# Stick-breaking attention on one core: TensorE's order written by hand, scores on row halves, masks by TensorE, the sample's queries on partitions

## The chip, the cores and the metric

One core of one Trainium2 chip runs the whole kernel in one launch. The metric is the device time of that launch in microseconds, the median of three runs. All inputs and outputs are float32.

## The reference, cut to what matters

One inference step of a two-layer encoder, for 256 prompt tokens and 32 sample tokens that have a cache of 256 past tokens. D is 1024. Layer 0 mixes with attentions A and B, layer 1 with C; behind each mixer come cross-attention into 256 memory tokens and an MLP of 4096. The change is in C, stick-breaking attention with 16 heads of 64:

```python
def stick_breaking_attend(q, k, v, q_pos, k_pos):
    z = jnp.einsum('bqhd,bkhd->bhqk', q, k) * (HEAD_DIM ** -0.5)
    before = k_pos[None, :] < q_pos[:, None]
    log_keep = jnp.where(before, jax.nn.log_sigmoid(-z), 0.0)
    tail = lax.cumsum(log_keep, axis=3, reverse=True) - log_keep
    w = jnp.where(before, jnp.exp(jax.nn.log_sigmoid(z) + tail), 0.0)
    return jnp.einsum('bhqk,bkhd->bqhd', w.astype(v.dtype), v)

# prompt: q, k, v = split(rmsnorm(h) @ sb_w_in, 3); 256 queries over 256 keys
# sample: 32 queries over the 256 cached keys and the 32 new ones
# then both: h = h + o @ sb_w_out
```

With `sp = softplus(z)`, both kernels use `w = exp(z - (sum of sp over this key and all later ones up to the query))`.

## The kernel before, in words

**Layout and products.** Activations lie transposed, features on the 128 partitions and the T = 288 tokens (256 prompt, 32 sample) along the free dimension, as 8 tiles of 128 features. A weight matrix comes in chunks of 256 columns and all 1024 rows, by two 512 KB loads on SP's queue (`load_chunk`). Each weight is split in two float32r parts: `wh`, a copy by ScalarE (L144) or VectorE (L142), and `wl = raw - wh` on VectorE or POOL (L145). One instruction of either does a piece of STEP[0] row tiles of 256 columns; every STEP[1]th piece's `wl` goes to POOL, every STEP[2]th piece's `wh` to VectorE (0: none). The activations are split likewise into `xh` and `xl` (L197 for the second), and each product is three matmuls, `mm3`: xh·wh (L159), xl·wh (L160), xh·wl (L161). A chunk is 48 of these, 24 into each of two PSUM banks `g` (pool `ps_g`, three banks). There are 960 products of 288 or 256 columns between the first product of layer 1's mixer and its output projection's last: 12 chunks of queries, keys and values, 4 of memory keys for the cross-attention, 4 of the output projection. Other PSUM pools in this stage are `ps_t`, one bank, and `R.s`, four banks `za`, `zb`, `zs`.

**The stage.** Heads are taken in 4 groups of 4; a group has two pairs of heads, one pair on the 128 partitions of a feature tile (head 0 on partitions 0 to 63, head 1 on 64 to 127). `project_qk` makes a group's `qz` and `kT`, scaled by the norm's `rs` as they leave PSUM. `qz` holds each pair twice, with the other head's rows at zero (`m8` is 0.125 on one half of the partitions), so that one matmul on all 128 rows gives one head's scores. `project_v` makes `vT` and turns it (L433, three transposes a pair into `ps_vt` in `ps_t`) into `vt`, keys on partitions, by two copies on ScalarE (L435, L436).

**Attention, prompt** (`attend_c`, for each pair). `qz` and `kT` are split into float32r parts, and the scores are three products of the parts: L578 into `za` (key tile 0, both heads, 512 columns), L579 into `zb` (key tile 1, queries 128 to 255 only, 256 columns). Softplus: Abs, Exp, Ln on ScalarE (L546, L548, L549), then max(z, 0) + that on VectorE (L553). POOL puts zeros where the key isn't before the query (L558). The result is split (`sph` L594, `spl` L596), and the sum over later keys is made by matmuls with `mtrir` (-1 at and below the diagonal) and `monesr` (all -1), added onto the scores that still lie in PSUM (L599 to L601). Exp gives `w` (L603), POOL masks it again, and L473 multiplies it with `vt`, each head on one half of the columns. `put_prompt` splits the result into `oh` and `ol` for the output projection.

**Attention, sample** (once a group). The scores have the keys on partitions: L618 for the two tiles of cached keys, L621 for the 32 new ones, into `zs`. The same softplus on 256 and 128 columns, the mask on POOL, the sum by plain float32 matmuls (L628 to L632), Exp to `ws` (L637), and `pv_sample` (L483).

**What sets the order.** The body calls the steps of the table `ORD_C` one after the other: `M` is `mem_split` (the split of the memory's activations for layer 1), `q`, `p`, `a` are `project_qk`, `project_v`, `attend_c` of a group, `K` is `mem_k`, a head's memory keys with their norm. `TileContext` then schedules the instructions of each engine by a timeline of its own, so the order on the engines is not that of the calls: products stand between attention steps where its timeline put them. Each engine runs its own queue in that order.

Of the kernel before, what the change touches and what calls it, by code (L numbers as in the profile page):

```python
# [8 lines left out]
F32 = mybir.dt.float32  # L9
F32R = mybir.dt.float32r  # L10
# [4 lines left out]
P = 128  # L15
NP_ = 256
# [15 lines left out]
SHE = 0  # L32
ORD_AB = 'qA0 pA0 F qA1 pA1 aA0 qB0 aA1 qB1 M pB0 pB1 aB0 K2 aB1 K0 K3 K1'.split()
ORD_C = 'M q0 q1 p0 a0 q2 p1 a1 q3 p2 a2 p3 a3 K0 K1 K2 K3'.split()
# [4 lines left out]
ZR = 1  # L39
QZB = (3, 3)  # L40
# [5 lines left out]
STEP = {'ab': (2, 4, 0), 'x0': (4, 5, 7), 'm0': (1, 5, 6), 'c': (2, 5, 0), 'x1': (2, 2, 3), 'm1': (2, 5, 0)}  # L46
# [6 lines left out]
def body(ctx: ExitStack, tc: tile.TileContext, i: dict, o: dict):  # L53
# [27 lines left out]
    def phase(kind):  # L81
        if R.stack is not None:
            R.stack.close()
        R.stack = ExitStack()
        R.step, R.pool_every, R.dve_every = STEP[kind]
        R.c = int(kind == "c")
        R.ph = R.stack.enter_context(tc.tile_pool(name="ph_" + kind, bufs=1))
        R.s = R.stack.enter_context(tc.tile_pool(name="s_" + kind, bufs=4 if kind[0] == "c" else 2, space=PS))
        R.m, R.o = ps_t, R.s
# [177 lines left out]
    eye32 = const.tile([P, NS], F32, name="eye32")  # L267
    for a in range(4):
        r = slice(32 * a, 32 * a + 32)
        dve.tensor_copy(eye32[r, :], ident[r, r])  # L270
        dve.tensor_copy(smask[r, NP_:T], bmask[r, P + 32 * a:P + 32 * a + 32])
# [10 lines left out]
    dve.tensor_copy(bdr, bd)  # L282

# [62 lines left out]
    def mem_k(layer, hd, mh, ml):  # L346
# [41 lines left out]
    def project_qk(wname, cq, ck, xh, xl, rs, norm, ko, oidx, ws0=None):  # L388
        qz = R.ph.tile([P, 2, 2, T], F32, tag="qz", name="qz", bufs=QZB[R.c])
        kT = R.ph.tile([P, 2, T], F32, tag="kT", name="kT", bufs=KTB[R.c])  # L390
        for which, chunk in ((0, cq), (1, ck)):
            ws = load_chunk(i[wname][chunk]) if ws0 is None or which else ws0
            pss = gemm2(ws, xh, xl, pool=R.s if FIRST_S and ws0 is not None and not which else ps_g)
            for p in range(2):
                ps = pss[p]
                if norm is None:
                    if which == 0:
                        for par in range(2):
                            dve.scalar_tensor_tensor(qz[:, p, par, :], ps[:, 0:T], m8[:, par:par + 1], rs,
                                                     ALU.mult, ALU.mult)  # L400
# [17 lines left out]

    def project_v(wname, cv, xh, xl, rs, vo, oidx):
# [7 lines left out]
        for p in range(2):  # L427
# [3 lines left out]
            pt = bank(ps_t, "ps_vt")  # L431
            for j in range(2):
                nc.tensor.transpose(pt[:, j * P:(j + 1) * P], vT[:, p, j * P:(j + 1) * P], ident)  # L433
            nc.tensor.transpose(pt[0:NS, 2 * P:3 * P], vT[:, p, NP_:T], ident)
            act(vt[:, 0:2, p * P:(p + 1) * P], pt[:, 0:2 * P].rearrange("p (j c) -> p j c", j=2), AF.Copy)  # L435
            act(vt[0:NS, 2, p * P:(p + 1) * P], pt[0:NS, 2 * P:3 * P], AF.Copy)  # L436
# [104 lines left out]
    def softplus(zs, w, a):  # L541

        c0 = 0
        for z in zs:
            c1 = c0 + z.shape[1]
            act(a[:, c0:c1], z, AF.Abs)  # L546
            c0 = c1
        act(a, a, AF.Exp, scale=-1.0)  # L548
        act(a, a, AF.Ln, bias=1.0)  # L549
        c0 = 0  # L550
        for z in zs:
            c1 = c0 + z.shape[1]
            dve.scalar_tensor_tensor(w[:, c0:c1], z, 0.0, a[:, c0:c1], ALU.max, ALU.add)  # L553
            c0 = c1

    def below_diag(x, pattern):

        nc.gpsimd.affine_select(x, x, pattern=pattern, compare_op=ALU.is_gt, fill=0.0, base=0,  # L558
                                channel_multiplier=-1)

    def attend_c(g, qz, kT, vt, ck, cv, oh, ol):
        kt0 = 2 * g
        k_ = dict(start=False, skip_group_check=True)
        for p in range(2):

            za = bank(R.s, "za")
            zb = bank(R.s, "zb")
            za2 = za.rearrange("p (e q) -> p e q", e=2)
            if ZR:
                qh = R.ph.tile([P, 2, NP_], F32R, tag="qh", name="qh")  # L570
                ql = R.ph.tile([P, 2, NP_], F32R, tag="ql", name="ql")
                kh = R.ph.tile([P, NP_], F32R, tag="kh", name="kh")
                kl = R.ph.tile([P, NP_], F32R, tag="kl", name="kl")
                split_into(kh, kl, kT[:, p, 0:NP_])
                split_into(qh, ql, qz[:, p, :, 0:NP_])
                f_ = True
                for x, y in ((kh, qh), (kh, ql), (kl, qh)):
                    mm(za2, x[:, 0:P], y, start=f_, stop=False, skip_group_check=True)  # L578
                    mm(zb[:, 0:NP_], x[:, P:NP_], y[:, :, P:NP_], start=f_, stop=False, skip_group_check=True)  # L579
                    f_ = False  # L580
            else:
                mm(za2, kT[:, p, 0:P], qz[:, p, :, 0:NP_], start=True, stop=False, skip_group_check=True)
                mm(zb[:, 0:NP_], kT[:, p, P:NP_], qz[:, p, :, P:NP_], start=True, stop=False, skip_group_check=True)
            a = R.ph.tile([P, 768], F32, tag="a", name="a", bufs=2)
            sp = R.ph.tile([P, 768], F32, tag="pr", name="sp", bufs=4)
            softplus([za, zb[:, 0:NP_]], sp, a)
            dia = [[0, 2], [1, P]]
            below_diag(sp[:, 0:512].rearrange("p (e q) -> p e q", e=2)[:, :, 0:P], dia)
            below_diag(sp[:, 512:768].rearrange("p (e q) -> p e q", e=2), dia)
            sh = R.ph.tile([P, 768], F32R, tag="a", name="sph", bufs=2)  # L590
            if SHE:
                dve.tensor_copy(sh, sp)
            else:
                act(sh, sp, AF.Copy)  # L594
            sl = R.ph.tile([P, 768], F32R, tag="pr", name="spl", bufs=4)
            dve.tensor_tensor(sl, sp, sh.bitcast(F32), ALU.subtract)  # L596
            for x, end in ((sh, False), (sl, True)):
                xb = x[:, 512:768]
                mm(za, mtrir, x[:, 0:512], stop=False, **k_)  # L599
                mm(za2[:, :, P:NP_], monesr, xb.rearrange("p (e q) -> p e q", e=2), stop=end, **k_)  # L600
                mm(zb[:, 0:NP_], mtrir, xb, stop=end, **k_)  # L601
            w = R.ph.tile([P, 768], F32, tag="pr", name="w", bufs=4)
            act(w[:, 0:512], za, AF.Exp)  # L603
# [8 lines left out]
        z = bank(R.s, "zs")
        fl = True
        for p in range(2):
            q = qz[:, p, :, NP_:T]
            for kk in range(2):
                c0 = kk * P + p * 64
                mm(z[:, c0:c0 + 64], ck[:, p, kk * P:(kk + 1) * P], q, start=fl, stop=False, skip_group_check=True)  # L618
                fl = False
            c0 = 2 * P + p * 64  # L620
            mm(z[0:NS, c0:c0 + 64], kT[:, p, NP_:T], q, start=False, stop=False, skip_group_check=True)  # L621
        a = R.ph.tile([P, 768], F32, tag="a", name="as_", bufs=2)
# [5 lines left out]
        mm(z[:, 0:2 * P], mtri, sp[:, 0:2 * P], stop=False, **k_)  # L628
        mm(z[:, 0:P], mones, sp[:, P:2 * P], stop=False, **k_)
        for c0 in (0, P):  # L630
            mm(z[:, c0:c0 + P], mones[0:NS, :], n3, stop=False, **k_)
        mm(z[0:NS, 2 * P:384], mtri[0:NS, 0:NS], n3, stop=True, **k_)  # L632
# [4 lines left out]
        act(w3, z[0:NS, 2 * P:384], AF.Exp)  # L637
# [379 lines left out]
```

## Time and profile before

| | us |
|---|---|
| runs, median | 975.23 (972.88 to 976.21, 3 runs) |
| the profiled execution | 970.67 |
| its span | 969.0, mean granted clock 0.993 |
| layer 1's mixer with its output projection | 494 to 667 of the span |

The profile is of one execution. PE is TensorE's matmul stream and PEld its weight loads, DVE VectorE, ACT ScalarE, POOL GpSimd, SP the engine that issues the large loads. L12 is line 12 of the kernel. The table of stretches has, after the time and its length, each engine's busy time with its count of instructions, then the granted clock of TensorE as a share of full speed. Waits read "waiting instruction <- what it waited for: sum, count, longest". Rows of the chain of waits read start, us on the path, engine, tile and line; groups of instructions have the count, then busy time and mean ns of one, then the idle time ahead of them and what ended it.

Shares of the whole span: TensorE 99%, VectorE 70%, ScalarE 56%, POOL 26%.

### The profile page before, as it was taken

How to read it: one execution, taken by the hardware profiler on the slowest of the kernel's cores; microseconds unless marked ns; L12 is line 12 of the kernel's file. 1: busy time of each engine (PE TensorE's matmuls, PEld its weight loads, DVE VectorE, ACT ScalarE, POOL GpSimd, SP SyncE). 2: the span in 40 equal slices, each digit the busy share in tenths (PEclk: the TensorE clock that was granted, in tenths of full speed). 3: DMA queues.
4: the chain of work that ended last, by engine and by line, in shares of the span. 5: the costliest groups of instructions: out<-in, count | busy, mean ns of one | idle time of the engine just before them, and what ended most of it. 6: DMA issues, size and time to landing. Idle time of an engine off the chain costs nothing.

```text
span 969.0 us, 19373 instructions
## 1 busy us (share of the span) xinstructions
PE 955.4 (99%) x7276; PEld 922.2 (95%) x7276; DVE 681.5 (70%) x1460; ACT 541.6 (56%) x1268; POOL 249.2 (26%) x291
## 2 busy tenths in 40 slices
PE   8999989999999999999999999999999999999998
PEld 8998878999999999999999999989999999999998
DVE  8788848879678767776695656778977766464643
ACT  6667647656456645444474677865554655454531
POOL 4311472221212211121122322323543112121110
PEclk8999998999999999999999999999999999999999
DMA  8654353754555555555566444356443455555452
GB/s 264 200 173 162 116 198 112 245 167 141 170 170 171 161 168 166 162 170 163 168 197 207 142 142 152 100 196 200 139 157 127 153 175 169 162 167 169 160 174 72
DMA packets 50702, 160.03 MB, mean 165 GB/s; under 512 B 6296, under 2 KB 12968, under 8 KB 50352
## 3 DMA queue, kind: packets, MB, share of 16 engines
q1 hardware_dynamic: 46864, 148.69, 47.9%
q0 software_dynamic: 2592, 8.92, 2.4%
q10 hardware_dynamic: 1152, 1.18, 0.4%
q8 instruction: 57, 0.93, 0.4%
q14 instruction: 37, 0.30, 0.1%
HBM read 148.65 MB, written 10.12 MB: 164 GB/s over the span
## 4 chain that ended last, share of the span: by engine, by line
PE 91%; DMA 3%; DVE 3%; issue 2%; POOL 1%; ACT 0%; SPq 0%; DVEq 0%; ACTq 0%; POOLq 0%
PE g L159 27%; PE g L161 27%; PE g L160 26%; DVE wl L145 1%; DMA raw<-in_w_kv_dram 1%; DMA bsmp<-cd 1%; PE za L473 1%; PE za L578 1%; DMA b<-cd 1%; PE zs L618 0%; PE s L516 0%; POOL b L844 0%; PE sx L159 0%; PE po L473 0%; PE za L599 0%
## 5 line engine op out<-in xcount | busy, mean ns | idle before, releaser
L144 ACT ACTIVATE wh<-raw 128x512 fp32r<-128x512 f32 (+3 forms) x561 | 279.8, 550 | 234.2 <-PE g L160 116.3
L145 DVE TENSOR_TENSOR wl<-raw,wh 128x512 fp32r<-128x512 f32 (+3 forms) x483 | 315.7, 687 | 113.7 <-ACT wh L144 107.5
L145 POOL TENSOR_TENSOR wl<-raw,wh 128x512 fp32r<-128x512 f32 (+2 forms) x141 | 175.0, 1241 | 530.8 <-ACT wh L144 430.7
L159 PE MATMUL g<-xh,wh 128*128 128x288 f32 (+1 forms) x1032 | 303.1, 298 | 1.1 <-ACT wh L144 0.7
L161 PE MATMUL g<-xh,wl 128*128 128x288 f32 (+1 forms) x1032 | 302.9, 298 | 1.3 <-DVE wl L145 1.2
L160 PE MATMUL g<-xl,wh 128*128 128x288 f32 (+1 forms) x1032 | 303.8, 297 | 0.0
L161 PEld LDWEIGHTS g<-xh,wl 128*128 128x128 f32 (+1 forms) x1032 | 193.0, 188 | 4.0 <-DVE wl L145 2.6
L159 PEld LDWEIGHTS g<-xh,wh 128*128 128x128 f32 (+1 forms) x1032 | 192.5, 188 | 2.7 <-ACT wh L144 0.9
L160 PEld LDWEIGHTS g<-xl,wh 128*128 128x128 f32 (+1 forms) x1032 | 193.4, 188 | 0.9 <-DVE xl L197 0.2
L160 PE MATMUL g<-hl,wh 128*128 128x288 f32 x512 | 150.3, 295 | 0.0
L159 PE MATMUL g<-hh,wh 128*128 128x288 f32 x512 | 148.9, 295 | 0.0
L161 PE MATMUL g<-hh,wl 128*128 128x288 f32 x512 | 148.5, 294 | 0.0
L160 PEld LDWEIGHTS g<-hl,wh 128*128 128x128 f32 x512 | 96.1, 188 | 0.0
L161 PEld LDWEIGHTS g<-hh,wl 128*128 128x128 f32 x512 | 95.7, 188 | 0.0
L159 PEld LDWEIGHTS g<-hh,wh 128*128 128x128 f32 x512 | 95.3, 187 | 0.0
L160 PE MATMUL g<-ol,wh 128*128 128x288 f32 x256 | 75.0, 295 | 0.0
L161 PE MATMUL g<-oh,wl 128*128 128x288 f32 x256 | 74.3, 295 | 0.0
L159 PE MATMUL g<-oh,wh 128*128 128x288 f32 x256 | 73.7, 295 | 0.3 <-ACT oh L492 0.3
L774 DVE TENSOR_TENSOR h<-h,g 128x288 f32<-128x288 f32 x64 | 28.8, 449 | 29.6 <-PE g L161 29.5
L161 PEld LDWEIGHTS g<-oh,wl 128*128 128x128 f32 x256 | 47.9, 188 | 0.4 <-issue 0.4
L160 PEld LDWEIGHTS g<-ol,wh 128*128 128x128 f32 x256 | 48.0, 188 | 0.0
L764 ACT ACTIVATE squ<-tu 128x288 f32<-128x288 f32 x64 | 27.9, 437 | 35.8 <-DVE tu L762 35.7
(313 smaller groups left out, 1525.2 us busy)
## 6 DMA issues: line engine op xcount, KB each, us to landing
raw<-in_w_up_dram SPq DMA_DIRECT2D x64, 512.0 KB, 3.8
raw<-in_w_down_dram SPq DMA_DIRECT2D x64, 512.0 KB, 3.8
raw<-in_w_kv_dram SPq DMA_DIRECT2D x32, 512.0 KB, 4.0
raw<-in_sb_w_dram SPq DMA_DIRECT2D x24, 512.0 KB, 4.8
raw<-in_ab_w_dram SPq DMA_DIRECT2D x22, 512.0 KB, 4.8
raw<-in_w_q_dram SPq DMA_DIRECT2D x16, 512.0 KB, 4.6
raw<-in_w_o_dram SPq DMA_DIRECT2D x16, 512.0 KB, 4.0
raw<-in_ab_wo_dram SPq DMA_DIRECT2D x8, 512.0 KB, 4.9
```

What stands on the lines that cost most here:

```text
L144: act(wh[:, r, :], src, AF.Copy)
L145: e.tensor_tensor(wl[:, r, :], src, wh[:, r, :].bitcast(F32), ALU.subtract)
L159: mm(out, lh, rh, start=first, stop=False)
L160: mm(out, lh, rl, start=False, stop=False)
L161: return mm(out, ll, rh, start=False, stop=last)
L473: mm(po[64 * par:64 * par + 64, kk * P:NP_], vt[:, kk, cols], pts[par][kk], start=kk == 0, stop=kk == 1)
L578: mm(za2, x[:, 0:P], y, start=f_, stop=False, skip_group_check=True)
L764: act(sq, t, AF.Square)
L774: dve.tensor_tensor(h[:, kt, :], h[:, kt, :], ps[:, 0:T], ALU.add)
```

## The change

**Order.** `ORD_C` now has chunks as steps (q, k, v, and m for memory keys). A generator `Mix` works through it and gives out products in pieces of 6 or 12; `attend_c` calls `fill(96)` between its scores and its cumulative sums and `fill(30)` between these and the values, and `until(...)` brings what it needs next. All this stands in `tc.manual_schedule` for TensorE, whose instructions then stay as called; the other engines are still scheduled. The two transpose sets of a group's values come 18 and 36 products after its value chunk, the norm of memory keys 36 after theirs. `mem_split` is called after q1 in place of ahead of q0.

**Prompt scores.** Plain float32 on row halves: head e's 64 rows of `kT` against the same rows of `qz`, which loses its zeroed half. A pair's scores lie in a `zz` tile of two banks, one a head, in three blocks of 128 columns with the two diagonal ones side by side. The mask is a matmul of `big` (2^100 on the diagonal) with `mtrir`, added onto the scores, so that softplus and Exp give zero there; POOL's selects are gone. The cumulative sums are eight matmuls a pair in place of six.

**Sample.** Queries lie on partitions (4 heads by 32), the 288 keys along the free dimension: scores L680 and L681 with `qs` (the sample's queries with the other head's rows zeroed, made on ScalarE), a mask `notbelow` (built in the prologue) for the new keys, and softplus on 128x288. The sum over later keys is a reversed scan on VectorE, `z` minus it goes through Exp, and three transposes and a copy (`wts`) put the weights back with keys on partitions for `pv_sample`.

**Weights.** STEP for this stage goes from (2, 5, 0) to (2, 2, 4): every second piece's `wl` on POOL instead of every fifth, every fourth `wh` on VectorE.

```diff
-ORD_C = 'M q0 q1 p0 a0 q2 p1 a1 q3 p2 a2 p3 a3 K0 K1 K2 K3'.split()
+ORD_C = 'q0 k0 v0 q1 M k1 v1 q2 m0 k2 v2 q3 k3 v3 m1 m2 m3'.split()
+FILL_C = 96, 30
-QZB = (3, 3)
+QZB = (3, 2)
-STEP = {... 'c': (2, 5, 0), ...}
+STEP = {... 'c': (2, 2, 4), ...}
...
-        R.s = R.stack.enter_context(tc.tile_pool(name="s_" + kind, bufs=4 if kind[0] == "c" else 2, space=PS))
+        R.s = R.stack.enter_context(tc.tile_pool(name="s_" + kind, bufs=2, space=PS))
...
     for a in range(4):
         r = slice(32 * a, 32 * a + 32)
         dve.tensor_copy(eye32[r, :], ident[r, r])
+        dve.scalar_tensor_tensor(nb_[r, :], mtri_[r, r], 1.0, ident[r, r], ALU.add, ALU.add)
...
+    dve.tensor_scalar(notbelow, nb_, -1.0, None, ALU.mult)
+    dve.tensor_scalar(m01, m8, 8.0, None, ALU.mult)
...
+    class Mix:
...
+        def fill(self, n):
+            while n > 0:
+                c = next(self.gen, 0)
+                if not c:
+                    break
+                n -= c
+                self.due(c)
...
+        def products(self, ap, xh, xl, n=T):
+            ws = load_chunk(ap)
+            ps = [bank(ps_g, "g") for _ in range(2)]
+            for k0, k1 in ((0, 1), (1, 2), (2, 4), (4, 6), (6, 8)):
+                for d in range(2):
+                    for k in range(k0, k1):
+                        wh, wl = ws[k]
+                        cols = slice(d * P, d * P + P)
+                        mm3(ps[d][:, 0:n], wh[:, cols], wl[:, cols], xh[:, k, 0:n], xl[:, k, 0:n], k == 0, k == KT - 1)
+                yield 6 * (k1 - k0)
+            self.ps = ps
...
+                elif op == "v":
...
+                    self.later(18, lambda turn=turn: turn(0))
+                    self.later(36, lambda turn=turn: turn(1))
+                else:
+                    yield from self.products(i["w_kv"][1, g], *mem, NP_)
...
-    def attend_c(g, qz, kT, vt, ck, cv, oh, ol):
+    def attend_c(g, qz, kT, vt, ck, cv, oh, ol, fill):
...
+        for par in range(2):
+            act(qs[:, :, par, :], qz[:, :, NP_:T], AF.Copy, scale=m01[:, par:par + 1])
...
         for p in range(2):
-            za = bank(R.s, "za")
-            zb = bank(R.s, "zb")
-            za2 = za.rearrange("p (e q) -> p e q", e=2)
-                split_into(kh, kl, kT[:, p, 0:NP_])
-                split_into(qh, ql, qz[:, p, :, 0:NP_])
-                for x, y in ((kh, qh), (kh, ql), (kl, qh)):
-                    mm(za2, x[:, 0:P], y, ...)
-                    mm(zb[:, 0:NP_], x[:, P:NP_], y[:, :, P:NP_], ...)
+            zz = R.s.tile([P, 2, 512], F32, tag="zz", name="zz")
+            for kk in range(2):
+                for e in range(2):
+                    r = slice(64 * e, 64 * e + 64)
+                    mm(block(zz, e, kk), kT[r, p, kk * P:(kk + 1) * P], qz[r, p, kk * P:NP_].rearrange("p (b c) -> p b c", c=P),
+                       start=kk == 0, stop=False, skip_group_check=True)
+            for e in range(2):
+                mm(zz[:, e, P * (1 - e):P * (3 - e)], big, mtrir.unsqueeze(1).to_broadcast([P, 2, P]), stop=False, **k_)
...
+            mm(dst[:, 0:NP_], q, ck[:, p, :], start=True, stop=False, skip_group_check=True)
+            mm(dst[:, NP_:T], q, kT[:, p, NP_:T], start=False, stop=False, skip_group_check=True)
+        mm(zp[:, NP_:T], big, notbelow, stop=True, **k_)
...
+        dve.tensor_copy(z, zp[:, 0:T])
...
+        dve.tensor_tensor_scan(su[:, ::-1], sps[:, ::-1], sps[:, ::-1], 0.0, ALU.add, ALU.max)
+        dve.tensor_tensor(ws[:, 0:T], z, su, ALU.subtract)
+        act(ws[:, 0:T], ws[:, 0:T], AF.Exp)
+        fill(FILL_C[0])
...
+        for kk in range(3):
+            nc.tensor.transpose(pp[:, kk * P:(kk + 1) * P], ws[:, kk * P:(kk + 1) * P], ident)
+        act(pt, pp[:, 0:384], AF.Copy)
+        fill(FILL_C[1])
+        vt = vt()
...
+    with tc.manual_schedule(engines={mybir.EngineType.PE}):
+        for g in range(4):
+            qz, kT = mix.until(("q", g)), mix.until(("k", g))
+            mix.fill(12)
+            attend_c(g, qz, kT, lambda g=g: mix.until(("v", g)), *caches("cckT", "ccv", g), oh, ol, mix.fill)
+        mix.fill(1000)
```

On TensorE, before, the sample's scores of group 0 stand among its prompt values (products left out of the rows):

```order
L618 MATMUL zs<-qz,ck 128x64 x2
L621 MATMUL zs<-qz,kT 32x64
L618 MATMUL zs<-qz,ck 128x64
L473 MATMUL za<-w,vt 64x256 x2
L473 MATMUL za<-w,vt 64x128 x2
L618 MATMUL zs<-qz,ck 128x64
L621 MATMUL zs<-qz,kT 32x64
```

Now a group's two pairs of scores, their masks and the sample's scores stand in one block, ahead of its 96 products:

```order
L671 MATMUL zz<-qz,kT 128x2x128 x2
L671 MATMUL zz<-qz,kT 128x128 x2
L674 MATMUL zz<-mtrir,big 128x256 x2
L671 MATMUL zz<-qz,kT 128x2x128 x2
L671 MATMUL zz<-qz,kT 128x128 x2
L674 MATMUL zz<-mtrir,big 128x256 x2
L680 MATMUL zs<-ck,qs 64x256
L681 MATMUL zs<-kT,qs 64x32
L680 MATMUL zs<-ck,qs 64x256
L681 MATMUL zs<-kT,qs 64x32
L682 MATMUL zs<-notbelow,big 128x32
```

The sample's matmuls on TensorE have moved from the values to the scores, and its cumulative sum has no row there any more. On ScalarE, before, the first value copies (`vt`) of a group stand among the Abs, Exp and Ln of one pair's softplus:

```order
L546 ACTIVATE a<-za 128x512
L546 ACTIVATE a<-zb 128x256
L179 ACTIVATE qh<-qz 128x512
L548 ACTIVATE a<-a 128x768
L435 ACTIVATE vt<-ps_vt 128x2x128
L436 ACTIVATE vt<-ps_vt 32x128
L549 ACTIVATE a<-a 128x768
```

Now they stand behind the softplus of both pairs and of the sample (L698 is Ln, `zsb` the sample's, `sph` the split), with three weight pieces (L143) between:

```order
L693 ACTIVATE zsb<-zsb 128x288
L698 ACTIVATE a<-a 128x768
L703 ACTIVATE sph<-sp 128x768
L695 ACTIVATE zsb<-zsb 128x288
L143 ACTIVATE wh<-raw 128x512 x2
L703 ACTIVATE sph<-sp 128x768
L698 ACTIVATE zsb<-zsb 128x288
L143 ACTIVATE wh<-raw 128x512
L432 ACTIVATE vt<-ps_vt 128x2x128
L433 ACTIVATE vt<-ps_vt 32x128
L432 ACTIVATE vt<-ps_vt 128x2x128
L433 ACTIVATE vt<-ps_vt 32x128
```

The copies moved from between two steps of one pair to the end of the whole block. On VectorE, the prologue's last two `xl` stood behind these rows before:

```order
L145 TENSOR_TENSOR wl<-raw,wh 128x256
L197 SCALAR_TENSOR_TENSOR xl<-h,gT,xh 128x288
L145 TENSOR_TENSOR wl<-raw,wh 128x256
L213 TENSOR_TENSOR ssum<-ssum,sq 128x288
L287 TENSOR_TENSOR qg<-qkg,m_128 128x1 x4
L197 SCALAR_TENSOR_TENSOR xl<-h,gT,xh 128x288
L289 TENSOR_SCALAR xg<-xqkg 128x4
```

and stand behind these now:

```order
L196 SCALAR_TENSOR_TENSOR xl<-h,gT,xh 128x288
L144 TENSOR_TENSOR wl<-raw,wh 128x256
L273 SCALAR_TENSOR_TENSOR nb<-mtri,ident 32x32 x4
L212 TENSOR_TENSOR ssum<-ssum,sq 128x288
L292 TENSOR_TENSOR qg<-qkg,m_128 128x1 x4
L276 TENSOR_SCALAR notbelow<-nb 128x32
L196 SCALAR_TENSOR_TENSOR xl<-h,gT,xh 128x288
L294 TENSOR_SCALAR xg<-xqkg 128x4
```

The five small steps of `nb` and `notbelow` came in ahead of the last `xl`; `m01` is made in the prologue too.

More of the change, by code (lines that the diff above doesn't have):

```diff
@@ L417, in project_qk, with turn_v @@
         return qz, kT
+    def turn_v(vT, vt, p):
+        pt = bank(ps_t, "ps_vt")
+        for j in range(2):
+            nc.tensor.transpose(pt[:, j * P:(j + 1) * P], vT[:, p, j * P:(j + 1) * P], ident)
+        nc.tensor.transpose(pt[0:NS, 2 * P:3 * P], vT[:, p, NP_:T], ident)
+        act(vt[:, 0:2, p * P:(p + 1) * P], pt[:, 0:2 * P].rearrange("p (j c) -> p j c", j=2), AF.Copy)
+        act(vt[0:NS, 2, p * P:(p + 1) * P], pt[0:NS, 2 * P:3 * P], AF.Copy)
     def project_v(wname, cv, xh, xl, rs, vo, oidx):
@@ L430, in project_v @@
                 dve.tensor_tensor(vT[:, p, :], ps[:, 0:T], rs, ALU.mult)
[L431 to L436, printed above, removed]
+            turn_v(vT, vt, p)
         nc.gpsimd.dma_start(out=o[vo][:, 2 * oidx:2 * oidx + 2, :], in_=vT)
@@ L538, in attend_ab @@
         put_sample(oh, ol, kt0, po)
[L541 to L559, printed above, removed]
@@ L612, in attend_c @@
[L612 to L622, printed above, removed]
@@ new lines, in attend_c @@
+        zp = bank(ps_t, "zs")
+        for p in range(2):
+            dst = zp[64 * p:64 * p + 64, :]
+            q = qs[:, p, :, :]
+            mm(dst[:, 0:NP_], q, ck[:, p, :], start=True, stop=False, skip_group_check=True)
+            mm(dst[:, NP_:T], q, kT[:, p, NP_:T], start=False, stop=False, skip_group_check=True)
+        mm(zp[:, NP_:T], big, notbelow, stop=True, **k_)
+        zt = R.ph.tile([P, 2, T], F32, tag="zsb", name="zsb")
+        z, su = zt[:, 0, :], zt[:, 1, :]
+        sps = R.ph.tile([P, T], F32, tag="sps", name="sps")
@@ new lines, in attend_c @@
+        ws = R.ph.tile([P, 384], F32, tag="ws", name="ws")
+        dve.tensor_copy(z, zp[:, 0:T])
+        nc.gpsimd.memset(ws[:, T:384], 0.0)
+        three = [(zz[:, :, 0:384], tile_a("a"), tile_p("sp")) for zz in zzs] + [(z, su, sps)]
+        for zv, a, sp in three:
+            act(a, zv, AF.Abs)
+        for zv, a, sp in three:
+            act(a, a, AF.Exp, scale=-1.0)
+        for zv, a, sp in three:
+            act(a, a, AF.Ln, bias=1.0)
+            dve.scalar_tensor_tensor(sp, zv, 0.0, a, ALU.max, ALU.add)
@@ new lines, in attend_c @@
+        parts = []
+        for zv, a, sp in three[0:2]:
+            sh, sl = tile_a("sph", F32R), tile_p("spl", F32R)
+            act(sh, sp, AF.Copy)
+            dve.tensor_tensor(sl, sp, sh.bitcast(F32), ALU.subtract)
+            parts.append((sh, sl))
+        dve.tensor_tensor_scan(su[:, ::-1], sps[:, ::-1], sps[:, ::-1], 0.0, ALU.add, ALU.max)
+        dve.tensor_tensor(ws[:, 0:T], z, su, ALU.subtract)
+        act(ws[:, 0:T], ws[:, 0:T], AF.Exp)
+        fill(FILL_C[0])
+        wps = []
@@ new lines, in attend_c @@
+        for zz, x2 in zip(zzs, parts):
+            for x, end in zip(x2, (False, True)):
+                for e in range(2):
+                    mm(zz[:, e, 0:384], mtrir, x[:, e, :], stop=False, **k_)
+                    mm(block(zz, e, 0)[:, 1, :], monesr, block(x, e, 1)[:, 0, :], stop=end, **k_)
+            w = tile_p("w")
+            act(w, zz[:, :, 0:384], AF.Exp)
+            wps.append(w)
+        pp = bank(ps_t, "ps_ws")
+        for kk in range(3):
+            nc.tensor.transpose(pp[:, kk * P:(kk + 1) * P], ws[:, kk * P:(kk + 1) * P], ident)
@@ L886, in body @@
     phase("c")
+    big = R.ph.tile([P, P], F32R, tag="big", name="big")
     oh = spp.tile([P, KT, T], F32R, tag="sp", name="oh1")
     ol = spp.tile([P, KT, T], F32R, tag="sp", name="ol1")
[L889 to L901 removed]
+    dve.tensor_scalar(big, ident, 2.0 ** 100, None, ALU.mult)
+    mix = Mix(ORD_C)
+    mix.x = xh, xl, rs
+    with tc.manual_schedule(engines={mybir.EngineType.PE}):
[4 more added lines that the diff above has]
+        mix.fill(1000)
+    mk1 = {g: mix.until(("m", g)) for g in range(4)}
+    mh, ml = mix.mem
     out_proj(i["sb_wo"], oh, ol)
```

157 lines of the change are left out of this document (78 added, 79 removed).

## The prediction, made before the changed kernel ran

> **What bounds the kernel now.** I read the page first, then the table of stretches, then who waits for whom on TensorE, then the chain of waits piece by piece.
>
> ```profile
> span 969.0 us, 19373 instructions
> PE 955.4 (99%) x7276; PEld 922.2 (95%) x7276; DVE 681.5 (70%) x1460; ACT 541.6 (56%) x1268; POOL 249.2 (26%) x291
> ...
> core 0: us, PE busy (x) PEld busy (x) DVE busy (x) ACT busy (x) POOL busy (x), PEclk, DMA share, GB/s
> 494.00:667.00 173.00, 172.06 (x1348) 161.71 (x1348) 117.77 (x218) 115.12 (x253) 49.55 (x75) 1.00 0.51 165
> ...
> PE zs L483 <- ACT ws L637: 0.6, 1, 0.6
> PE g L159 <- ACT oh L492: 0.3, 1, 0.3
> ```
>
> The stage that the change touches (layer 1's mixer with its output projection) lies between 494 and 667 us of the span. TensorE is busy in it for 172.06 of 173 us at the full granted clock; the last two rows are all that it waits for there, 0.9 us. VectorE and ScalarE are at 68% and 67%. So no wait is left to remove: the stage gets shorter only by what leaves TensorE's own stream, and longer by each wait that a fixed order puts in. How that stream divides, the chain of waits says:
>
> ```profile
> by line: PE g L159 24.7%; PE g L161 24.6%; PE g L160 24.4%; PE za L473 4.0%; PE za L578 3.4%; PE zs L618 2.6%; PE za L599 2.3%; PE zs L483 2.0%; PE zb L579 1.9%; PE zs L631 1.5%; PE ps_vt L433 1.2%; PE zs L628 1.1%; PE zb L601 1.1%; PE za L
> ```
>
> The weight products (L159 to L161) take 73.7% of 173 us, 127.5 us, and the change keeps every one. The remaining 45 us are attention, and that is the whole field.
>
> **What leaves TensorE.** Prices are steps of the chain (start, us on the path, what), since busy times of pipelined matmuls overlap. Here are group 0's sample rows and one set of score rows.
>
> ```profile
> 545.29 0.39 PE zs L618 x4
> 545.68 0.23 PE zs L621 x2
> 545.91 0.36 PE zs L618 x2
> ...
> 547.08 0.37 PE zs L618 x2
> 547.45 0.23 PE zs L621 x2
> ...
> 555.48 0.43 PE zs L628 x2
> 555.91 0.22 PE zs L629 x2
> 556.14 0.64 PE zs L631 x4
> 556.77 0.33 PE zs L632 x2
> ...
> 561.32 0.90 PE za L578 x3
> ...
> 565.13 0.36 PE zb L579 x3
> ```
>
> The sample's scores and its cumulative sum cost 0.39+0.23+0.36+0.37+0.23 + 0.43+0.22+0.64+0.33 = 3.20 us a group, 12.8 us in four. The prompt's split scores are L578 and L579, 3.4% and 1.9% of 173 us: 9.2 us. The sample's cumulative sum goes to a VectorE scan, so the 0.6 us that TensorE waited at the end (L483 for ScalarE's `ws`) goes too. Out: 12.8 + 9.2 + 0.6 = 22.6 us.
>
> **What comes onto TensorE.** These rows are of layer 0, where the same shapes in plain fp32 run, and of a fragment like the new ones.
>
> ```profile
> 53.12 0.59 PE ss L505 x4
> ...
> 57.95 0.22 PE ps_vt L433 x2
> 58.28 0.43 PE s L516 x2
> 58.72 0.22 PE s L517 x2
> ...
> 546.28 0.80 PE za L473 x8
> ```
>
> - Scores, eight pairs of heads. Each pair has four fp32 matmuls of 256, 256, 128 and 128 columns on 64 rows. On the full array a 256 and a 128 cost 0.43 + 0.22 = 0.65 us (L516, L517, two passes each). If the two row halves run side by side the four cost 0.65, one after the other 1.30. No row shows row halves. The nearest is L473: the same eight passes of the same lengths on the two column halves, 0.80. I take that: 8 x 0.80 = 6.4 us (5.2 to 10.4).
> - Masks: 16 matmuls of 256 fp32r columns at 0.12 (L579, 0.36 for three): 1.9 us.
> - Sample: scores like L505, 0.59, the 32 new columns 0.1 (estimate: an eighth of L505), a 32-column mask between 0 and 0.12, say 0.1: 0.8 a group, 3.2 us. Three transposes at 0.11 (L433): 0.33 a group, 1.3 us.
> - The prompt's cumulative sums keep their 2048 columns a pair, in eight matmuls for six; I take 0. Sixteen more matmuls at most 0.11 each bound it by 1.8 us.
>
> In: 6.4 + 1.9 + 3.2 + 1.3 = 12.8 us. Values, value transposes and head norms keep count and size. TensorE's stream gets 9.8 us shorter.
>
> [...]
>
> ```profile
> L618 PEld LDWEIGHTS zs<-qz,ck 128*128 128x128 f32 x32 | 4.5, 189 | 1.6 <-issue 1.3
> ...
> L631 PEld LDWEIGHTS zs<-sps,monesr 32*128 32x128 f32 x16 | 2.1, 185 | 0.5
> ```
>
> That is 185 ns for 32 rows and 189 for 128. [...]
>
> **What comes back as waits.** TensorE's order is now fixed in the stage, so a late operand stops all products behind it. I walked one group through the order of the engines with these rows:
>
> ```profile
> L144 ACT ACTIVATE wh<-raw 128x512 fp32r<-128x512 f32 x81 | 46.8, 623 | 27.7 <-PE g L160 19.3 <-POOL wl L145 2.6 <-issue 2.6
> L145 POOL TENSOR_TENSOR wl<-raw,wh 128x512 fp32r<-128x512 f32 x17 | 24.1, 1418 | 59.0 <-ACT wh L144 52.4 <-DVE wh L142 3.8 <-PE g L161 2.9
> L596 DVE TENSOR_TENSOR spl<-sp,sph 128x768 fp32r<-128x768 f32 x8 | 8.1, 1008 | 2.1 <-ACT sph L594 2.1
> L548 ACT ACTIVATE a<-a 128x768 f32<-128x768 f32 x8 | 6.7, 840 | 0.0
> L594 ACT ACTIVATE sph<-sp 128x768 fp32r<-128x768 f32 x8 | 6.7, 832 | 1.8 <-POOL sp L558 1.8
> L430 DVE TENSOR_TENSOR vT<-g,rs 128x288 f32<-128x288 f32 x8 | 3.6, 451 | 5.8 <-PE g L161 5.8
> L435 ACT ACTIVATE vt<-ps_vt 128x256 f32<-128x256 f32 x8 | 3.0, 381 | 0.2
> L436 ACT ACTIVATE vt<-ps_vt 32x128 f32<-32x128 f32 x8 | 2.0, 251 | 0.0
> ...
> ACT wh L144 <- PE g L160: 19.3, 18, 2.8
> ```
>
> - The first pair's scores are done at time 0. ScalarE then runs six 128x768 steps (Abs, Exp, Ln twice, about 0.84 each, 5.0), one copy `sph` 0.83, two 288-wide sample steps 0.9 (estimate: 288/768 of 0.84 and a fixed part), two weight pieces 1.25, the second `sph` 0.83, the last sample step 0.45, one more piece 0.62: 9.9 us. Only then the first value copy, 0.38 + 0.25: 10.5. TensorE gets there after the second pair 1.0, the sample 0.8, 48 products 6.4 (0.133 each: 127.5 us for 960), a transpose set 0.33 and 12 products 1.6: 10.1. [...]
> - The chain to the cumulative sums (`spl` of the second pair, at 10.9) has 96 products, the sample, the transposes and that wait as cover: TensorE asks at about 16. If the cover were gone the chain would cost 5 us a group more. `w` (ready 3 us before its use) has 30 products. The scan feeds only the transposes at the end of the same cover; a scan of 288 took 0.72 us:
>
> ```profile
> L815 DVE TENSOR_TENSOR_SCAN c<-lf,zer x1: 720/720/720, 40.5 to 40.5; 8x288 f32<-8x288 f32 x1
> ```
>
> - Three banks of `g`: the second half of chunk k0 needs q0's first bank, freed by `qz`, which waits for the norm. `qz` started 2.1 us after L216 here:
>
> ```profile
> 501.04 0.48 PE ps_rs L216 x2
> ...
> 503.17 1.37 DVE L399 SCALAR_TENSOR_TENSOR qz<-g,m,rs 128x288 f32<-128x288 f32 x3
> ```
>
>   Before, the scheduler let the first half run on alone; now the order forbids it. The norm stands 8 products earlier, so 11 products (1.5 us) cover 2.1: 0.6 us once, of which I take 0.4, since ScalarE was on a weight piece when the norm came.
> - `mem_split`, moved from the end of the MLP into the first group: eight copies on ScalarE, eight on VectorE and two loads on SP behind eight of `sb_w`. They end before the first scores are read (ScalarE has 12 us for 10 us of work); with that cover gone they would cost 3 us, once.
> - POOL loses its selects and gets every second weight piece:
>
> ```profile
> L558 POOL TENSOR_SCALAR_AFFINE_SELECT w<-w 128x256 f32<-128x256 f32 x16 | 7.8, 507 | 8.0 <-ACT w L603 8.0
> L558 POOL TENSOR_SCALAR_AFFINE_SELECT sp<-sp 128x256 f32<-128x256 f32 x16 | 7.6, 497 | 3.1 <-DVE sp L553 3.0
> ```
>
>   These two groups are 15.4 of its 49.6 us; about 40 pieces at 1.42 for 17 add 33, so some 67 us of 166. VectorE has 25 pieces fewer. In my walk a piece is needed 3 us or more after its copy: nothing.
> - Prologue: six small VectorE steps before the last two `xl`:
>
> ```profile
> L271 DVE COPY smask<-bmask 32x32 f32<-32x32 f32 x4 | 0.7, 171 | 0.0
> ```
>
>   0.9 us on an engine that then feeds TensorE: 0 to 0.9, I take 0.4.
>
> Back: 2.8 + 0.4 + 0.4 = 3.6 us. **Sum:** -22.6 + 12.8 + 3.6 = -6.2 us. The profiled execution took 970.67 us (1.7 more than its span): 964.5. It stands 4.6 us under the median of the three runs, 975.23; against that median it is 969.0.
>
> **Rivals.**
> - *All hides*: scores at 0.65 (-1.2), no wait at the value transpose (-2.8). For it: ScalarE misses by 0.4 us in my walk. Against: a strict queue with three weight pieces ahead. 975.2 - 10.2 = 965.
> - *Row halves run one after the other*: scores 10.4, +4.0, so -2.2: 973. For it: no row shows them overlapping. Against: L473's column halves do. [...]
> - *ScalarE's queue holds TensorE up, slower*: ScalarE idled 27.7 us here, 19.3 of it with weight pieces that waited for TensorE to free a slot (the last row: 18 times, at most 2.8 us). Before, TensorE did something else meanwhile; now such a piece stands ahead of the value copy. The piece there waits for the product just before the first transpose set; in my walk it is reached 1.2 us after that. If ScalarE is that much ahead, or VectorE late, each group can lose the longest wait more: 4 x 2.8 = 11.2, so +5: 980. It decides from 1.6 us more a group on. That the change doesn't do what it says is excluded by the order of the built program.
>
> **How the numbers follow.** My forecast 0.45, all hides 0.20, no row overlap 0.18, ScalarE's queue 0.17. 969.0 is the likeliest case's; its own range is 966 to 972. From 962 (all hides with the prologue free and no hand-over) to 976 (no row overlap and the cumulative sums at their bound) 0.8 is held; what is left out is mostly the slower case. No change can be told within 0.3%, 2.9 us. Faster: 0.45 + 0.20 + a little of the third, 0.67; same 0.16 (most of the third); slower 0.17.
>
> **What would show it.** Right: the score rows of a pair at 0.7 to 0.9 us on the chain; the sample's scores near 0.7 a group; a wait of 0.5 to 1 us at the second value transpose for ScalarE's `vt`, four times; none at the cumulative sums; the stage at about 166 us. Wrong: score rows of 1.3; TensorE waiting more than 2 us a group for ScalarE or VectorE, above all for `spl`, `w` or `wl`; a lower granted clock in the stage.

## The result, and the profile after

The changed kernel is slower: 979.46 us (977.61 to 980.09, 6 runs) against 972.96 for the kernel before on the same chip, a ratio of 1.0064 (95% interval 1.0044 to 1.0084). Run once more beside other kernels it gave 979.09, 1.0070 (1.0046 to 1.0094). The forecast was 969, faster; it was worked out from 975.23 us, the median of the three runs of the kernel before that were on record then.

The page of the changed kernel's profile, its span and its engines:

```profile
span 976.1 us, 19332 instructions
PE 952.5 (98%) x7284; PEld 920.4 (94%) x7284; DVE 691.8 (71%) x1439; ACT 524.8 (54%) x1212; POOL 266.8 (27%) x275
```

TensorE works 2.9 us less than before (955.4), and the span is 7.1 us longer. The table of stretches says where. Here is the stage from the first product of layer 1's mixer to the first one behind its output projection, before:

```profile
494.49:666.34 171.85, 170.91 (x1340) 160.56 (x1339) 116.62 (x215) 114.53 (x251) 49.55 (x75) 1.00 0.51 166
```

and after:

```profile
498.97:673.44 174.47, 165.41 (x1348) 157.05 (x1347) 123.67 (x191) 100.29 (x202) 64.94 (x57) 1.00 0.50 164
```

The stage starts 4.5 us later, and lasts 2.6 us longer although TensorE is busy for 5.5 us less. So it stands idle for 9.1 us where it stood for 0.9. What it waits for there:

```profile
PE zz L494 <- DVE ol L499: 3.9, 4, 1.6
PE g L158 <- DVE qz L607: 2.8, 3, 1.0
PE g L158 <- DVE tmk L637: 1.6, 1, 1.6
PE g L158 <- DVE kT L613: 0.7, 1, 0.7
```

L494 is the sample's values, L158 the first product that reuses a bank of `g`; all four rows wait for VectorE. With the time from each TensorE instruction's start to the next one's, added up by kind over the stage (idle time taken out), the account is: attention 44.2 before, 36.0 after; products 126.7 and 129.4; idle 0.9 and 9.1. That is -8.2 + 2.7 + 8.2 = +2.7 us, the stage's 2.6 but for rounding.

One group's scores, on the chain of waits (start, us on the path, what):

```profile
516.89 0.85 PE zz L671 x8
517.75 0.43 PE zz L674 x2
...
519.46 0.59 PE zs L680 x4
520.05 0.09 PE zs L681 x4
520.14 0.21 PE zs L682
```

The four score matmuls of a pair take 0.85 us, its two masks 0.43, the sample's scores 0.68 and its mask 0.21.

### The profile page after: what moved, and what is told of

Its sections match the earlier page's. It is cut to its first block, busy times and chain, and to the rows that moved or that the text cites. A ratio compares the mean times of both kernels' runs of the same rounds, so it can differ in the third digit from the quotient of the medians.

```text
span 976.1 us, 19332 instructions
## 1 busy us (share of the span) xinstructions
PE 952.5 (98%) x7284; PEld 920.4 (94%) x7284; DVE 691.8 (71%) x1439; ACT 524.8 (54%) x1212; POOL 266.8 (27%) x275
## 5 line engine op out<-in xcount | busy, mean ns | idle before, releaser
L143 ACT ACTIVATE wh<-raw 128x512 fp32r<-128x512 f32 (+3 forms) x541 | 269.2, 547 | 234.0 <-PE g L159 107.6
L144 DVE TENSOR_TENSOR wl<-raw,wh 128x512 fp32r<-128x512 f32 (+3 forms) x459 | 309.6, 707 | 99.4 <-ACT wh L143 94.5
L144 POOL TENSOR_TENSOR wl<-raw,wh 128x512 fp32r<-128x512 f32 (+2 forms) x165 | 209.1, 1268 | 532.8 <-ACT wh L143 410.6
L158 PE MATMUL g<-xh,wh 128*128 128x288 f32 (+1 forms) x1032 | 305.0, 299 | 2.9 <-DVE qz L607 1.8
L158 PEld LDWEIGHTS g<-xh,wh 128*128 128x128 f32 (+1 forms) x1032 | 192.9, 188 | 5.0 <-DVE qz L607 2.6
L158 PE MATMUL g<-hh,wh 128*128 128x288 f32 x512 | 149.0, 295 | 0.0
L158 PEld LDWEIGHTS g<-hh,wh 128*128 128x128 f32 x512 | 95.3, 187 | 0.0
L158 PE MATMUL g<-oh,wh 128*128 128x288 f32 x256 | 74.1, 295 | 0.0
L141 DVE CAST wh<-raw 128x256 fp32r<-128x256 f32 (+2 forms) x83 | 31.9, 384 | 46.3 <-PE g L159 24.5
```

The costliest lines, as they stand in the source:

```text
L141: dve.tensor_copy(wh[:, r, :], src)
L143: act(wh[:, r, :], src, AF.Copy)
L144: e.tensor_tensor(wl[:, r, :], src, wh[:, r, :].bitcast(F32), ALU.subtract)
L158: mm(out, lh, rh, start=first, stop=False)
```

## The experiments

Each ratio is against the kernel before, on the same chip. The stage is that of the one profiled execution, from the first product of the mixer to the first behind the output projection.

| kernel | median us | ratio (95%) | stage | idle in it |
|---|---|---|---|---|
| before | 972.96 | 1 | 171.9 | 0.9 |
| changed | 979.46 | 1.0064 (1.0044 to 1.0084) | 174.5 | 9.1 |
| changed, again | 979.09 | 1.0070 (1.0046 to 1.0094) | 176.0 | 9.1 |
| masks built late | 976.2 | 1.0035 (1.0020 to 1.0049) | 176.1 | 9.1 |
| before, with the masks' steps | 974.73 | 1.0024 (1.0009 to 1.0038) | 173.4 | 0.9 |
| spacing 12 and 12 | 975.21 | 1.0026 (1.0012 to 1.0040) | 172.3 | 7.1 |
| own bank for the sample's values | 971.54 | 0.9992 (0.9976 to 1.0009) | 169.4 | 5.1 |
| mask tile | 976.97 | 1.0041 (1.0022 to 1.0061) | 174.4 | 9.0 |
| scheduler's order | 970.14 | 0.9981 (0.9969 to 0.9993) | 167.2 | 0.9 |
| scan behind the eviction | 975.84 | 1.0038 (1.0022 to 1.0053) | 173.6 | 6.5 |
| all edits, order by hand | 968.88 | 0.9965 (0.9949 to 0.9982) | 168.4 | 2.6 |
| scheduler's order, two edits | 968.37 | 0.9955 (0.9938 to 0.9972) | 167.1 | 0.9 |

Five of these stages hold one window of 3.4 us at half clock each (last section), an estimated 1.7 us by half of its length, where 1.6 was measured: the changed kernel's again, masks built late, before with the masks' steps, scan behind the eviction, all edits.

**The prologue.** Masks built late:

```diff
-    (in the prologue) nb, notbelow, m01
+    masks()          # the same six steps, from mtrir
     mlp(0, xh, xl, rs)
```

> The six small VectorE steps of the prologue (four for nb, notbelow, m01) are built ahead of layer 0's MLP instead; nothing else changes, and the order of layer 0 on TensorE is then that of the kernel before. Theory: these steps alone delay xl and with it layer 0, so the first product of layer 1's mixer, at 499.0 us in the changed kernel, comes back to 494.5 (4.4 us), and the time falls from 979.5 to about 975. Rival: the delay in layer 0 is the scatter of one execution or has another source; the first product stays at 499 and the time within 1 us of 979.5.

The counterpart, the kernel before with these six steps in its prologue:

> The kernel before with only the six small VectorE steps added to its prologue (their results are used by nothing). Theory: the first product of layer 1's mixer moves from 494.5 to 499.0 us and the kernel takes about 4.4 us more than before, 977.4. Rival: layer 0 is as before, 973.

The time of the first is about 3 us under the changed kernel's, that of the second 2.3 over the kernel before. But the first product of the mixer stood at 496.84 and 496.80 us, neither where the theory nor where the rival had it: this mark scatters by some us between executions (498.97 and 500.79 in two of the changed kernel). A steadier one is the 145th product, in layer 0's first group. It stood at 33.9 to 34.5 us in nine executions with the steps and at 31.8 to 32.8 in four without (means 34.0 and 32.3). So the steps cost 1.7 us, not 4.4. Most of the rest of the late start arises in one place, some 60 products behind the 500th: in the changed kernel's profiled execution TensorE waits there 1.9 us for VectorE's `mx` (0.4 before), and a window of half clock follows (107.4 to 110.8 us). This is not the six steps' doing: with them added to the kernel before, the wait was 0.4 us and no such window came, and the fastest kernel, which builds them late, waited 2.5. How 1.7 comes about, VectorE before:

```profile
14.40 0.36 DVE L287 TENSOR_TENSOR qg<-qkg,m 128x1 f32<-128x1 f32 x4
14.68 0.51 DVE L197 SCALAR_TENSOR_TENSOR xl<-h,gT,xh 128x288 fp32r<-128x288 f32 x1
```

and in the changed kernel:

```profile
14.05 0.76 DVE L273 SCALAR_TENSOR_TENSOR nb<-mtri,ident 32x32 f32<-32x32 f32 x4
...
15.50 0.18 DVE L276 TENSOR_SCALAR notbelow<-nb 128x32 fp32r<-128x32 f32 x1
15.59 0.51 DVE L196 SCALAR_TENSOR_TENSOR xl<-h,gT,xh 128x288 fp32r<-128x288 f32 x1
```

`xl` starts 0.91 us later, and the products behind it 0.7. The other 1.1 come some 60 products on: VectorE and ScalarE are late with the head norm, and TensorE waits for `sh` and `sl` (0.3 each) where it had both in time.

**The sample's values.** They go to the bank of `ps_t`:

```diff
-        po = zzs[1][:, 1, :]
+        po = bank(ps_t, "pos")
```

> The changed kernel, with the sample's values (L494) in the bank of ps_t instead of the second bank of the pair's zz tile. Theory: TensorE waits there for VectorE's ol of the pair's prompt values only because both lie in one tile; the four waits of 0.9, 1.6, 0.9 and 0.4 us go, time about 975.5. Rival: another operand (the copy wts, or the bank) is as late, and at least 2.5 of the 3.9 us stay; time above 978.

All four waits went; those for `qz` (2.8), `tmk` (1.6) and `kT` (0.6) stayed. The time fell by 7 us, to that of the kernel before, and the stage by 5.1 us, more than the 3.9 of idle time: the matmuls of the values took 8.5 us instead of 9.3, and the products 129.1 instead of 129.4. The other 2 us of the 7 do not lie in the stage, and this edit does not explain them.

The chain of the changed kernel shows what was there. The second pair's values end; then ScalarE's `oh` and VectorE's `ol` read them out of the first bank of `zz`; only then may the sample's values be written into its second bank:

```profile
541.60 1.48 PE zz L484 x16
...
543.10 0.39 ACT oh L498
...
543.51 0.43 DVE ol L499
...
543.99 0.89 PE zz L494 x24
```

**The evictions.** Spacing as in the kernel before:

```diff
-            for k0, k1 in ((0, 1), (1, 2), (2, 4), (4, 6), (6, 8)):
+            for k0, k1 in ((0, 1), (1, 2), (2, 4), (4, 8)):
```

> The changed kernel, with the products of a chunk in the spacing of the kernel before: the last four row tiles of one bank, then of the other (12 and 12), in place of two tiles of each in turn (6, 6, 6, 6). Counts and fills stay. Between the last product into a chunk's first bank and the product that reuses this bank there are then 15 products (2.0 us) instead of 9 (1.2 us). Theory: the six waits of TensorE's products for qz, kT and tmk, 5.2 us, with about 0.26 us each of slower products around them, shrink to 1 to 2 us in all; time about 975. Rival: the evictions are late by VectorE's queue (the sample's scan ahead of qz), so the waits stay above 3.5 us and the time above 978.

Its waits:

```profile
PE zz L494 <- DVE ol L499: 4.4, 4, 2.0
PE g L158 <- DVE qz L608: 1.6, 3, 0.9
PE g L158 <- DVE tmk L638: 1.0, 1, 1.0
```

The evictions' waits fell from 5.2 to 2.7 us (with one of 0.1 in each, too short for the list), between the two expectations; the one for `kT` went. `ol` took 0.5 back, and the stage got 2.2 us shorter. The other half of the cause is VectorE's queue, as the timeline of the changed kernel shows:

```profile
528.25 0.45 DVE L699 SCALAR_TENSOR_TENSOR sps<-zsb 128x288 f32<-128x288 f32 x1
...
528.46 1.38 POOL L144 TENSOR_TENSOR wl<-raw,wh 128x512 fp32r<-128x512 f32 x1 [1.29 <-issue]
...
528.62 1.77 DVE L144 TENSOR_TENSOR wl<-raw,wh 128x512 fp32r<-128x512 f32 x1
...
530.30 0.74 DVE L707 TENSOR_TENSOR_SCAN zsb<-sps 128x288 f32<-128x288 f32 x1
...
530.76 0.29 PE L160 MATMUL g<-xh,wl 128*128 128x288 f32 x1
531.09 0.46 DVE L708 TENSOR_TENSOR ws<-zsb 128x288 f32<-128x288 f32 x1
531.46 0.81 DVE L607 SCALAR_TENSOR_TENSOR qz<-g,rs 128x288 f32<-128x288 f32 x2
...
531.97 0.40 PE L158 MATMUL g<-xh,wh 128*128 128x288 f32 x1 [0.92 <-DVE qz L607]
```

The sample's scan and subtraction stand ahead of `qz` just when the chunk ends. That place recurs in all four groups, because the chunk ends 84 products (11.2 us) after the scores, and VectorE comes to the scan about then.

A second delay stands in the same rows. The scan's input `sps` was done at 528.70, but a weight piece came first, and beside a piece on POOL it took 1.77 us where others take 0.68 (last section). At 0.68 the scan and the subtraction would have been done 1.1 us earlier, an estimate from these two figures, and the wait was 0.92. In each of the other groups, too, a step that was stretched beside a POOL piece (1.5 to 1.8 us) stands ahead of the scan. The change had moved every second piece to POOL instead of every fifth. No run took this back, so its share in the waits is open.

The experiment puts the scan behind:

```diff
-        dve.tensor_tensor_scan(su[:, ::-1], ...)
-        dve.tensor_tensor(ws[:, 0:T], z, su, ALU.subtract)
-        fill(FILL_C[0])
+        fill(90)
+        with tc.issue_after(mix.evict.ins):
+            (scan and subtraction)
+        fill(FILL_C[0] - 90)
```

> The changed kernel, with the sample's scan and the subtraction behind it (0.74 and 0.46 us on VectorE) queued behind the eviction of the chunk that ends next to them (qz three times, tmk once), instead of ahead of it. Theory: this queue is what the four waits of 0.92, 0.95, 0.92 and 1.62 us are; they fall from 4.4 to about 1 us, with some 0.2 us each of slower products around them: time 978.4 - 4.2 = 974. Rival: three banks are too few for pieces of 6 whatever the queue; more than 2.5 us stay, time above 976.

Its waits, the three longest:

```profile
PE zz L494 <- DVE ol L499: 4.4, 3, 1.6
PE g L158 <- DVE tmk L637: 0.8, 1, 0.8
PE g L158 <- DVE kT L613: 0.7, 1, 0.7
```

The four waits fell from 4.4 to 0.9 us (0.8 for `tmk`; the three for `qz`, 0.14 together, are too short for the list). By the ratios the time fell by 2.5 to 3.1 us, less than the 4.2 expected: 0.5 came back each at `ol` and at the matmuls of norms and transposes. The remaining wait, for `kT`, has another cause. On the changed kernel's chain stand the load of the memory's activations, the memory split's `mh` and `ml` behind it, and then `kT`; no run moved the split:

```profile
508.58 3.78 DMA mraw<-in_memT_dram
...
512.39 0.52 ACT mh L311
512.93 0.48 DVE ml L312
513.42 0.38 DVE kT L613
513.84 0.40 PE g L158
```

**The masks.** A tile in place of a stride of zero:

```diff
-mtrir.unsqueeze(1).to_broadcast([P, 2, P])
+mtri2          # 2x128 columns
```

> The changed kernel, with the mask's moving operand a tile of 2x128 columns in place of one 128-column tile read twice through a stride of zero (two VectorE copies of 128x128 more at the stage's start). The mask rows (L674) took 0.216 us each on TensorE's stream, where fp32r matmuls of 256 columns took 0.12 before. Theory: the stride of zero costs the 0.1; rows of 0.12, 1.5 us of 16 rows gone, time about 977. Rival: it is the load of big, which nothing hides; rows stay at 0.21 and the time at 978.4.

The theory fell: two mask rows took 0.43 as before, and the stage was as long as before. That the time came out at the 977 it had named is chance. So the masks were grouped:

```diff
-            (two masks behind each pair's scores)
+        for zz in zzs:
+            (two masks each, behind the scores of both pairs)
```

> The changed kernel, with the four masks of a group behind the scores of both pairs instead of two behind each pair. A mask row takes 0.216 us on TensorE's stream, with a tile of its own as much as through a stride of zero. Theory: about 0.1 us is lost at each change between row-half matmuls and full ones, where the next weight load starts only with its matmul; with half the changes the sixteen mask rows fall from 3.45 to between 2.5 and 2.8 us. Rival: a mask row costs 0.216 wherever it stands (3.45 us).

On its chain:

```profile
514.51 1.51 PE zz L671 x16
516.01 0.68 PE zz L676 x4
```

Four masks take 0.68 instead of 0.86, all sixteen 2.70 instead of 3.45: those between two masks take 0.12, the first and last of a row about 0.1 more. This fits the theory of a price for each change between matmuls on halves of the array and on the whole array: the first weight load of the first pair's masks in the changed kernel starts within 0.01 us of its matmul (517.67 and 517.68), a product's 0.13 ahead (516.34 and 516.47). Products agree: one just ahead of a group's scores takes 0.22 us, one just ahead of its cumulative sums, which are on the whole array, 0.13. The single run was no faster for it (979.74; stage 178.3, idle 12.7 and one window of half clock). The first pair's softplus now starts 0.4 us later, and in the first group the second pair's `spl` (0.94 us) and a weight piece (0.68) then stood ahead of `qz` on VectorE. Its waits for the evictions of `qz` and `tmk`:

```profile
PE g L158 <- DVE qz L607: 5.6, 3, 1.9
PE g L158 <- DVE tmk L637: 2.4, 1, 2.4
```

**The order.** The new attention, with TensorE's order left to the scheduler:

```diff
-    with tc.manual_schedule(engines={mybir.EngineType.PE}):
+    with ExitStack():
```

> The changed kernel without the order written by hand: the calls stay, and the scheduler orders TensorE too. Theory (the waits are those of a fixed order): the scheduler puts ready work ahead of most of the 9.1 us of waits, so the stage falls from 174.5 to between 166 and 170, time 970 to 974. Rival (the new attention itself costs, or the waits are those of the tiles): gaps of 7 us or more stay, time 976 or more.

Its stretch, and the one wait in it:

```profile
497.54:664.77 167.23, 166.30 (x1349) 157.78 (x1347) 122.29 (x192) 99.67 (x202) 64.44 (x57) 1.00 0.52 171
```

```profile
PE g L158 <- DVE qz L607: 0.9, 1, 0.9
```

The stage is 7.3 us shorter than with the written order and 4.6 shorter than before; of 9.1 us of idle time 0.9 are left. On its chain, at the sample's values, the scheduler put other work between (products, left out here, and the next group's scores):

```profile
538.55 1.45 PE zz L484 x16
...
542.98 0.85 PE zz L671 x6
543.83 0.82 PE zz L494 x24
```

So the new attention is a gain, and the order written by hand is what turned it into a loss.

**Together.** All edits with the written order, then the scheduler's order with the late masks and the own bank:

> All edits together: prologue's steps late, spacing of 12 and 12, the sample's values in ps_t's bank, mask tile, scan behind the eviction. Theory: the gains add where they touch different waits: 978.4 - 1.4 (prologue) - 5.1 (sample's values, stage) - 4.5 (evictions) - 1.5 (masks) = 966, the stage at 163 to 164 us. Rival: late operands take each other's place and half of it is given back, 972 or more.

> The changed kernel with the scheduler's order for TensorE, the prologue's six steps late, and the sample's values in ps_t's bank. Theory: the scheduler's order gave 970.1 us with a stage of 167.2; the prologue gives 1.4 back and the bank little more, since no wait for ol was left there: 968 to 969, stage 166 to 167.5. Rival: the bank of ps_t, now shared by one more user, makes value transposes wait: stage 168 or more, 970 or more.

> The changed kernel once more, unchanged, so that the edits are compared with it on one chip. Both theories: 1.006 times the kernel before, stage 174.5 us with 9.1 us of waits of TensorE, plus 1.7 us for each window of half clock that happens to fall in it.

The first came to 968.88, between theory and rival. The mask tile gave nothing of its 1.5, a window of half clock (below) cost an estimated 1.7 in the profiled execution, and two waits for the memory keys' norm, 1.0 each, took the place of those removed. The second is the fastest, 968.37, with the stage as expected; the two can't be told apart.

## Why the prediction was wrong

What it said of TensorE's own work held in the main. The sample's scores and sums on keys, the split scores and the wait for `ws` are gone; counted from start to start the first took 13.7 us (12.8 priced), the second 9.3 (9.2). Row halves run side by side: their matmuls start 0.007 us apart, and a pair takes 0.85 us against 0.80 taken, so the rival of no overlap (1.30) is out. The sample's scores took 3.2 us as taken, the transposes 1.0 instead of 1.3. Masks were 3.5 instead of 1.9, at the changes between halves of the array and the whole. The cumulative sums, taken at 0 within a bound of 1.8, cost 1.4 more (9.0 against 7.6). The values gave 0.9 back, value transposes and head norms 0.2. In all -8.2 us where the terms said -9.2 (without the wait for `ws`). With the scheduler's order the stage came to 167.2 us, near the forecast 166.

The step that failed is "What comes back as waits", 3.6 us in all, 3.2 of them in the stage. There TensorE stood idle for 9.1 us, all of it behind VectorE, 2.3 us a group: a sign of being wrong that the prediction had named. Where its terms failed:

- The wait at the second value transpose, 2.8 us, did not occur. Of its 0.7 us a group the walk gives 0.4 (10.5 against 10.1). The other 0.3, for the passing from engine to engine, no run shows; on the chains of the changed kernel the next engine began 0.02 to 0.04 us after the one before it. ScalarE reached the first copy earlier than walked, and it ended 0.75 us before TensorE's next transposes at 528.58:

```profile
527.32 0.37 ACT L432 ACTIVATE vt<-ps_vt 128x256 f32<-128x256 f32 x1
527.58 0.25 ACT L433 ACTIVATE vt<-ps_vt 32x128 f32<-32x128 f32 x1
```

- The three banks of `g` were looked at in one place, chunk k0, where the norm was late (0.4 taken, 0.1 measured). At the end of each chunk the cover had fallen from 15 products to 9, and at four chunks VectorE had the scan ahead of the eviction. The prediction said the scan "feeds only the transposes" and did not ask what stands behind it: 4.4 us.
- "VectorE has 25 pieces fewer" was true (65 before, 40 after), but VectorE's load in the stage rose from 116.6 to 123.7 us: 20 weight copies came to it, 9.0 us, and its pieces took 1.12 us on average instead of 0.80, those beside a POOL piece 1.4 to 1.8. The prediction priced this at nothing; how much of the 4.4 us it explains is open.
- "Values ... keep count and size" was true, but their place in PSUM was not asked for: 3.9 us of idle time, 5.1 us of the stage.
- `mem_split` was taken as free because it ends before the scores; by the chain it delayed `kT` by 0.7 us before that, which no run tested.
- A wait was priced at its idle time. The product ahead of a wait takes 0.29 us and the one behind it 0.24 instead of 0.13. This makes 1.7 of the 2.7 us that the 960 unchanged products took more; the other 1.0 lies where products meet attention's matmuls. In the scheduler's order, with one wait in the stage, they still took 128.4 us against 126.7.
- The prologue was taken at 0.4 within 0 to 0.9. It cost 1.7, since the delay met a second chain, the head norm.

The slower rival had the right form, a strict order behind an engine that is late, and the wrong engine: it blamed ScalarE's queue, with VectorE in a clause, and gave it 0.17. That its 980 us lies near the 979.46 measured is luck. The prediction's rows of weight loads, 185 and 189 ns each, say little of the new scores: their loads took 186, an estimated 1.5 us for eight in a row, but a pair's eight lay in 0.73 us together. And the range was set wider than its terms give: for 962 and 976 they give 964.2 (no wait at all) and 974.8.

Stage (+2.6) and prologue (+1.7) make 4.3 of the 6.5 us. In the profiled execution the rest lies at the wait for `mx` in layer 0 and the window of half clock behind it; how it divides over the other executions isn't settled.

## What to carry to other kernels

When an order is fixed by hand, walk it once for every resource that is reused, not only for operands: for each bank, count the work between its last write and its next one, and read what stands ahead of the eviction in that engine's queue. Two results that are read out at different times belong in different PSUM tiles (here that took away 3.9 us of waits). Price a wait at more than its idle time (here 0.26 us more each), and keep small set-up steps off the engine that feeds the first products (six of them cost 1.7 us). Where work moves to POOL, count what VectorE's own pieces then take (1.42 to 1.80 us beside a POOL piece, 0.68 otherwise).

## What the runs showed of the hardware

TensorE's granted clock fell from 1.00 to 0.50 for 3.4 us after some waits and not after others of the same size. This is the same kernel at the same wait (1.6 us, second group's sample's values) in its two profiled executions, the stretch that holds the wait and the next one; the third column from the end is the granted clock. First:

```profile
571.60:575.00 3.40, 1.79 (x30) 1.26 (x30) 3.12 (x6) 1.44 (x4) 1.27 (x1) 1.00 0.13 47
575.00:578.40 3.40, 3.40 (x39) 3.36 (x36) 0.61 (x2) 0.62 (x2) 0.31 (x1) 1.00 0.61 185
```

Again:

```profile
574.40:577.90 3.50, 1.90 (x35) 1.57 (x31) 2.54 (x6) 0.82 (x3) 1.14 (x2) 1.00 0.40 124
577.90:581.30 3.40, 3.40 (x17) 3.40 (x16) 0.00 (x0) 0.00 (x0) 0.00 (x0) 0.50 0.34 108
```

Only 17 products fall in the second stretch there, where 25 fit at 0.133 us each, and the stage was 1.6 us longer (176.03 against 174.47) with the same waits. In the stage, 1.60 us of idle time or more within 3.4 to 3.5 us was followed by such a window in some executions only (1.60 here, 1.61 with the masks built late, 1.90 with all edits; not 1.61 in the first execution), and in one, before with the masks' steps, 0.94 was. What opens a window no run shows; ahead of this one TensorE was busy for 1.90 of 3.50 us. A wait of 1.6 us can thus cost 1.6 more.

VectorE's weight pieces took longer beside POOL's. In the stage, before:

```profile
L145 DVE TENSOR_TENSOR wl<-raw,wh 128x512 fp32r<-128x512 f32 x65 | 50.1, 795 | 20.5 <-ACT wh L144 19.2 <-issue 0.8
```

and after:

```profile
L144 DVE TENSOR_TENSOR wl<-raw,wh 128x512 fp32r<-128x512 f32 x40 | 44.8, 1121 | 4.0 <-ACT wh L143 4.0
```

Of these 40 pieces 23 took 0.68 to 0.69 us. The other 17 took 1.42 to 1.80, and just these ran beside a POOL piece for more than 0.8 us. Before, with 17 pieces on POOL instead of 40, 9 of the 65 took over 1 us, all of them beside a POOL piece.
